# A batch-norm matmul on one core: laying k so that each block of w is one DMA over all partitions, and moving three small products to GpSimd

## The chip, the cores and the metric

One core of a Trainium2 chip. The time is what the device takes for one execution, in microseconds (us), as the median of several. In what follows PE is the matmul engine, DVE the Vector engine, ACT the Scalar engine, GpSimd (POOL in the profile) the engine that also issues the loads of x and w.

## The reference

```python
# x: 16 x 512 x 1024 float32, weight: 1024 x 768
y = np.matmul(x, weight)
mean = np.mean(y, axis=(0, 1), keepdims=True)
var = np.var(y, axis=(0, 1), keepdims=True)
return gamma * (y - mean) / np.sqrt(var + eps) + beta
```

The statistics go over all 8192 rows, so nothing can be written before all of a column's products are there.

## The kernel before

x comes in 16 chunks of 512 rows, cast to bf16 by the DMA. A chunk is loaded in four slabs of 256 columns, each to 32 partitions; DVE then transposes blocks of 32x32 words, where a word is a pair of bf16 values. After that, partition `32 i + c` holds, in block `jw`, the pair of k values that starts at `256 i + 64 jw + 2 c`. w must lie the same way, and since the partition number has two parts with different steps (256 and 2), a block of w takes four DMAs:

```python
def load_w(jw, jw1):
    rows = weight.rearrange("(i jw c e) n -> i c jw (e n)", i=4, jw=JW, e=2)
    dst = w_sb.rearrange("p jw e n -> p jw (e n)")
    for i in range(4):
        seq(nc.gpsimd.dma_start(dst[32 * i:32 * i + 32, jw:jw1], rows[i, :, jw:jw1]))

def turn_x(m0, t0, jw0=0, jw1=JW):
    ...
    src = src.rearrange("p (t jw c) -> p t jw c", jw=JW, c=32)   # 32 words in a row
    ...
    seq(nc.vector.transpose(dst[:, half, :, jw0:jw1], src[:, :, jw0:jw1]))
```

For three of the six column groups most chunks are multiplied with x as the stationary operand (`mm_rows`, 128x384 results). Each such result is squared by ACT, added up by DVE (`add_rows`) and only then copied out by ACT (`keep_rows`), which frees its PSUM bank:

```python
def add_squares(c, s):
    eng, acc = (nc.vector, sum3) if s == RT - 1 and c < C - 3 else (nc.gpsimd, sum2)
    seq(eng.tensor_add(acc, acc, py.pop(("sq", c, s))))

def add_rows(c, s):
    seq(nc.vector.tensor_add(sum1, py["row", c, s][:, 0:NA], sum1))

def keep_rows(c, s):
    ...
    seq(nc.scalar.copy(yrow[c][:, s], py.pop(("row", c, s))[:, 0:NA]))
```

All instructions of an engine run in the order of the kernel's own list of events, so an event's planned time decides its place and nothing else.

## Time and profile before

| | before |
|---|---|
| time, median of 3 | 220.94 us |
| PE busy | 198.5 of 218.9 us |
| DVE busy | 155.7 us |
| a 1024-element transpose (30 of them) | 1.23 us |
| PE's first 128x384 matmul (end of the start) | 24.07 us |
| statistics of the first columns combined, at | 126.48 us |
| statistics of the last column group combined, at | 200.52 us |

The last three rows are landmarks: start, first pass, second pass. They are start times in the timelines of PE and DVE. The lines that show the bound are in the prediction below.

### The profile page before, as it was taken

What the parts mean: (1) busy time and instruction counts of PE and PEld (TensorE: products, weight loads), DVE (VectorE), ACT (ScalarE), POOL (GpSimd) and SP (SyncE); (2) the same over time, 40 slices, a digit from 0 to 9 for tenths busy, and PEclk for the clock granted to TensorE, in tenths of its full rate; (3) what the DMA queues carried; (4) which work ended last, traced back from release to release, by engine and by line L of the source; (5) the groups of instructions that cost most, each with busy time, mean ns of one, the idle gap of its engine ahead of it and who ended that gap; (6) DMA issues with size and microseconds to landing.
All of it is one profiled execution on the core that took longest, in us unless ns stands there. A gap on an engine that the chain in (4) does not pass through costs nothing.

```text
span 218.9 us, 3417 instructions
## 1 busy us (share of the span) xinstructions
PE 198.5 (91%) x1154; PEld 105.2 (48%) x1170; DVE 155.7 (71%) x264; ACT 119.8 (55%) x220; POOL 134.0 (61%) x153
## 2 busy tenths in 40 slices
PE   7998999999999999999999979999999988995900
PEld 3453545454544555546555534444444545651900
DVE  3223788897978789998554287889989999745800
ACT  2001454554543566636666225776676887985850
POOL 8897595977765799935559103999899953000000
PEclk9999999999999999999999999999999999999795
DMA  5999999999999999990000000986769899999698
GB/s 60 175 204 190 194 196 196 197 196 196 194 191 197 195 196 196 198 189 10 0 4 0 0 0 14 340 308 257 269 258 360 295 353 334 346 346 347 201 345 244
DMA packets 70161, 43.75 MB, mean 200 GB/s; under 512 B 4096, under 2 KB 69632, under 8 KB 70144
## 3 DMA queue, kind: packets, MB, share of 16 engines
q0 software_dynamic: 34624, 18.36, 61.1%
q1 hardware_dynamic: 35520, 25.18, 35.7%
q8 instruction: 9, 0.15, 0.3%
q14 instruction: 8, 0.07, 0.1%
HBM read 36.71 MB, written 25.17 MB: 283 GB/s over the span
## 4 chain that ended last, share of the span: by engine, by line
PE 64%; DVE 10%; POOL 8%; DMA 6%; issue 4%; ACT 3%; ACTq 0%; DVEq 0%; POOLq 0%
PE y_ps L190 31%; PE y_ps L180 29%; POOL ring L280 6%; PE o_ps L340 3%; ACT o_sb L353 3%; DVE stats L299 3%; DMA w_sb<-in_weight_dram 3%; DVE ring L274 2%; DVE y_sb L324 2%; DMA ring<-in_x_dram 2%; POOL w_sb L143 2%; DMA out_dram<-ring 1%; POOL ring L156 1%; DVE mv L306 1%; PE a_ps L266 1%
## 5 line engine op out<-in xcount | busy, mean ns | idle before, releaser
L190 PE MATMUL y_ps<-xT_sb,w_sb 128*128 128x512 bf16 (+1 forms) x477 | 117.5, 381 | 2.6 <-DMA w_sb<-in_weight_dram 1.4
L190 PEld LDWEIGHTS <-w_sb 128*128 128x128 bf16 x492 | 46.7, 96 | 60.8 <-issue 3.1
L302 ACT CAST y_sb<-y_ps 128x512 bf16<-128x512 f32 x60 | 35.4, 590 | 53.3 <-DVE stats L299 51.4
L180 PE MATMUL y_ps<-w_sb,xT_sb 128*128 128x384 bf16 x384 | 63.4, 326 | 0.0
L299 DVE BATCH_NORM_STATS2 stats<-y_ps 128x6 f32<-128x512 f32 x60 | 40.6, 684 | 22.5 <-PE y_ps L190 22.3
L280 POOL TENSOR_TENSOR ring<-ring,sum 128x768 f32<-128x768 f32 x24 | 43.5, 1847 | 17.9 <-ACT sum L268 14.0
L156 POOL DMA_DIRECT2D ring<-in_x_dram x72 | 45.2, 633 | 11.7 <-DVE xT_sb L168 6.1
L180 PEld LDWEIGHTS <-xT_sb 128*128 128x128 bf16 x384 | 37.5, 98 | 25.6
L206 POOL TENSOR_TENSOR sum<-sum,sq_sb 128x384 f32<-128x384 f32 x38 | 38.0, 1000 | 18.0 <-ACT sq_sb L202 16.8
L168 DVE STREAM_TRANSPOSE xT_sb<-ring 128x1024 f32<-128x1024 f32 (+1 forms) x34 | 39.5, 1167 | 12.0 <-DMA ring<-in_x_dram 12.0
L340 PE MATMUL o_ps<-ident,y_sb 128*128 128x128 bf16 x240 | 37.3, 230 | 5.5 <-DVE y_sb L324 5.2
L209 DVE TENSOR_TENSOR sum<-y_ps,sum 128x384 f32<-128x384 f32 x48 | 26.1, 544 | 14.6 <-ACT sq_sb L202 13.8
L202 ACT ACTIVATE sq_sb<-y_ps 128x384 f32<-128x384 f32 x48 | 23.4, 492 | 14.9 <-PE y_ps L180 11.4
L215 ACT CAST y_sb<-y_ps 128x384 bf16<-128x384 f32 x48 | 22.9, 476 | 7.5 <-DVE sum L209 7.3
L353 ACT CAST ring<-o_ps 128x1024 f32<-128x1024 bf16 (+1 forms) x24 | 22.5, 960 | 4.9 <-PE o_ps L340 2.5
L340 PEld LDWEIGHTS <-y_sb 128*128 128x128 bf16 x240 | 20.6, 104 | 9.1 <-DVE y_sb L324 7.3
L274 DVE TENSOR_TENSOR ring<-y_sb,a_ps 128x768 f32<-128x768 bf16 x24 | 22.3, 938 | 0.2 <-PE a_ps L266 0.2
L324 DVE TENSOR_SCALAR y_sb<-y_sb,scale,shift 128x512 bf16<-128x512 bf16 x43 | 17.3, 457 | 0.0
L319 ACT ACTIVATE y_sb<-y_sb,shift,scale 128x512 bf16<-128x512 bf16 x17 | 13.3, 813 | 0.1
L149 PE MATMUL idle_ps<-idle_sb 128*128 128x512 bf16 x37 | 9.8, 429 | 1.2 <-DVE idle_sb L100 1.2
L353 ACT CAST o_sb<-o_ps 128x512 f32<-128x512 bf16 x16 | 7.9, 679 | 1.2 <-PE o_ps L340 1.2
L149 PEld LDWEIGHTS <-idle_sb 128*128 128x128 bf16 x38 | 4.0, 108 | 6.4 <-issue 1.9
(45 smaller groups left out, 35.9 us busy)
## 6 DMA issues: line engine op xcount, KB each, us to landing
ring<-in_x_dram POOLq DMA_DIRECT2D x56, 256.0 KB, 8.5
out_dram<-ring SPq DMA_DIRECT2D x32, 384.0 KB, 2.9
out_dram<-ring SPq DMA_DIRECT2D x16, 512.0 KB, 5.9
out_dram<-o_sb SPq DMA_DIRECT2D x16, 256.0 KB, 3.3
ring<-in_x_dram POOLq DMA_DIRECT2D x16, 128.0 KB, 5.2
w_sb<-in_weight_dram POOLq DMA_DIRECT2D x8, 96.0 KB, 4.6
w_sb<-in_weight_dram POOLq DMA_DIRECT2D x4, 192.0 KB, 5.4
gamma_sb<-in_gamma_dram SPq DMA_DIRECT2D x6, 0.5 KB, 4.8
```

What stands on the lines that cost most here:

```text
L156: seq(nc.gpsimd.dma_start(x_bf[32 * i:32 * i + 32], src[:, :, KQ * i:KQ * (i + 1)]))
L168: seq(nc.vector.transpose(dst[:, half, :, jw0:jw1], src[:, :, jw0:jw1]))
L180: seq(nc.tensor.matmul(y_ps, xT[c][:, jw, s * P:(s + 1) * P, e], w_sb[:, jw, e, 0:NA], start=(jw == 0 and e == 0), stop=(jw == JW - 1 and ...
L190: seq(nc.tensor.matmul(y_ps, w_sb[:, jw, e, nt * P:(nt + 1) * P], xT[c][:, jw, q0 * QR:q1 * QR, e], start=(jw == 0 and e == 0 and q0 == 0) ...
L206: seq(eng.tensor_add(acc, acc, py.pop(("sq", c, s))))
L209: seq(nc.vector.tensor_add(sum1, py["row", c, s][:, 0:NA], sum1))
L274: seq(nc.vector.tensor_mul(o_sb, yrow[c][:, s:s + 2], aff[0][:, None, :].to_broadcast([P, 2, NA]),))
L280: seq(nc.gpsimd.tensor_add(o_sb, o_sb, sum1[:, None, :].to_broadcast([P, 2, NA])))
L299: seq(nc.vector.bn_stats(stats[:, nt, i, :], py[nt, c]))
L302: seq(nc.scalar.copy(y(nt, c), py.pop((nt, c))))
L340: seq(nc.tensor.transpose(dst, src, ident))
L353: seq(nc.scalar.copy(o_sb, src))
```

## The change

The intent: with k laid as `8 p + 2 jw + e`, the rows of w that partition p needs follow one another with a single step, so a block is one DMA over 128 partitions. In `turn_x` the 32 words that go to one block no longer lie side by side, but 4 words (16 bytes) apart. With fewer DMAs, blocks 2 and 3 of w are loaded and used one by one. Three 128x128 products move from DVE to GpSimd, and some norms move up by 1 us in the list.

```diff
     def load_w(jw, jw1):
-        rows = weight.rearrange("(i jw c e) n -> i c jw (e n)", i=4, jw=JW, e=2)
+        rows = weight.rearrange("(p jw e) n -> p jw (e n)", jw=JW, e=2)
         dst = w_sb.rearrange("p jw e n -> p jw (e n)")
-        for i in range(4):
-            seq(nc.gpsimd.dma_start(dst[32 * i:32 * i + 32, jw:jw1], rows[i, :, jw:jw1]))
+        seq(nc.gpsimd.dma_start(dst[:, jw:jw1], rows[:, jw:jw1]))
 ...
-        src = src.rearrange("p (t jw c) -> p t jw c", jw=JW, c=32)
+        src = src.rearrange("p (t c jw) -> p t jw c", jw=JW, c=32)
 ...  (shift_diag)
-            seq(nc.vector.tensor_scalar(
+            seq(nc.gpsimd.tensor_scalar(
 ...
-    order = [..., ("w", 1, 2), ("w", 2, 4)]
+    order = [..., ("w", 1, 2), ("w", 2, 3), ("w", 3, 4)]
 ...
-    pe = max(pe, arrive["w", 2])
+    part(2, 0, 2, [2])
+    pe = max(pe, arrive["w", 3])
     for nt in range(NT):
-        unit(nt, 0, MM_US / 2, [2, 3])
+        unit(nt, 0, MM_US / 4, [3])
 ...
-    at(S + 5.2, spread_rows, 1)
+    at(S + 5.0, spread_rows, 1)
 ...
-                at(tb - 2.2 + 0.5 * i, norm, ...)
+                at(tb - 3.2 + 0.5 * i, norm, ...)
```

More of the change, by code (lines that the diff above doesn't have):

```diff
@@ L372 @@
     arrive = {}
-    order = [("x", 0), ("w", 0, 1), ("x", 1), ("w", 1, 2), ("w", 2, 4)]
+    order = [("x", 0), ("w", 0, 1), ("x", 1), ("w", 1, 2), ("w", 2, 3), ("w", 3, 4)]
     order += [("x", q) for q in range(2, SHORT * QPC)] + [("c", c) for c in range(SHORT, C)]
@@ L377 @@
             at(t, load_w, n, *n1)
-            t += 2.1 * (n1[0] - n)
+            t += 1.6
             arrive["w", n] = t + 3.5
@@ L481, in outputs @@
             for i in range(2):
-                at(tb - 2.2 + 0.5 * i, norm, nt, 2 * b + i, "act" if tb < tr + 2.0 and i == 0 else "dve")
+                at(tb - 3.2 + 0.5 * i, norm, nt, 2 * b + i, "act" if tb < tr + 2.0 and i == 0 else "dve")
             at(tb, turn_y, (nt,), 2 * b * CH, 2 * RT)
```

## The prediction

> **What bounds the kernel now.** I first read the page's chain of waits (its shares by engine, then by line), to see which engine carries the end.
>
> ```profile
> PE 64%; DVE 10%; POOL 8%; DMA 6%; issue 4%; ACT 3%; ACTq 0%; DVEq 0%; POOLq 0%
> PE y_ps L190 31%; PE y_ps L180 29%; POOL ring L280 6%; PE o_ps L340 3%; ACT o_sb L353 3%; DVE stats L299 3%; DMA w_sb<-in_weight_dram 3%; DVE ring L274 2%; DVE y_sb L324 2%; DMA ring<-in_x_dram 2%; POOL w_sb L143 2%; DMA out_dram<-ring 1%; POOL ring L156 1%; DVE mv L306 1%; PE a_ps L266 1%
> ```
>
> TensorE's matmuls are the bound; the weight load (3% as DMA, 2% as its issue on GpSimd) is on the chain only at the start. Next, the busy time by stretches (columns: us; busy us and count of PE, PEld, DVE, ACT, POOL; granted clock; DMA share; GB/s).
>
> ```profile
> 13.00:18.70 5.70, 4.44 (x25) 2.21 (x25) 0.89 (x2) 0.00 (x0) 4.66 (x10) 1.00 1.12 201
> 18.70:24.00 5.30, 5.30 (x24) 2.25 (x25) 4.03 (x6) 1.93 (x4) 4.42 (x7) 1.00 1.44 193
> 24.00:45.00 21.00, 20.87 (x111) 10.75 (x111) 17.27 (x24) 10.48 (x23) 15.49 (x21) 1.00 1.45 197
> ...
> 72.00:93.00 21.00, 21.00 (x130) 12.60 (x130) 18.61 (x27) 13.40 (x30) 19.26 (x26) 1.00 1.45 197
> ...
> 126.00:132.00 6.00, 4.74 (x24) 1.83 (x22) 5.39 (x27) 1.35 (x3) 0.00 (x0) 1.00 0.00 0
> ```
>
> From 18.7 us on PE is full until the statistics are combined at 126. But DVE is not far behind: 17.27 of 21 us, then 18.61 of 21. Its slack there is what this change can break. What can be won lies before 18.7, so I read PE's timeline there (start, us, engine, line, what; in brackets the idle time before it and what ended it), and the groups of the two lines that change.
>
> ```profile
> 13.35 4.43 PE L190 MATMUL y_ps<-xT_sb,w_sb 128*128 128x256 bf16 x24 [0.44 <-DVE xT_sb L168]
> 18.66 5.58 PE L190 MATMUL y_ps<-xT_sb,w_sb 128*128 128x512 bf16 x24 [0.88 <-DMA w_sb<-in_weight_dram]
> ...
> L143 POOL DMA_DIRECT2D w_sb<-in_weight_dram x12: 492/508/542, 3.7 to 12.7; - x12
> ...
> L168 DVE STREAM_TRANSPOSE xT_sb<-ring x34: 669/1230/1246, 8.0 to 102.5; 128x1024 f32<-128x1024 f32 x30, 128x512 f32<-128x512 f32 x4
> ```
>
> PE starts the second quarter of x at 13.35, when its transpose is there, works 4.43 us, and then waits only 0.88 us for the last w blocks.
>
> **What the Trainium skill says.** (1) "SBUF — State Buffer", section "Door 1: The DMA port swizzle": SBUF has 16-byte lines, and an engine needs "≥2 hits per line to absorb SRAM access latency"; the same note says strides are free up to 4 fp32. For a stride of exactly 4 fp32, which this change makes, its two halves disagree: one access per line is under two hits, yet four elements is named as free. The trace before has no wide read with such a stride, so it can't decide. (2) The same page, "Who interferes with whom": a Vector instruction in a 2-port mode or with two SBUF inputs shares a port with GpSimd, and the second one waits. The trace agrees: line 312, a 128x1 multiply that takes 0.16 us at 201.66 us with GpSimd idle, takes 1.39 us at 152.02 while GpSimd adds. (3) "DMA: Bandwidth & Descriptors", "Rules for kernel authors": two transfers to disjoint partition halves share the same engines; use one over 128 partitions. That bears on the issue; whether the transfer gets faster no row here shows.
>
> **The change, part by part.**
>
> *Weight load.* Twelve issues of 0.508 us become four: 8 x 0.5 = 4 us less of GpSimd's time in the first 13 us. The program's order shows more: a DMA of GpSimd waits for the one issued eight before it. With fewer DMAs, the second quarter of x and the three later w blocks now wait only for pieces of the first x quarter, all landed by 7.9 us; the last w issue moves from 12.74 to about 8.5. But the landings in the trace show that the engines are already full by then: x0 lands at 7.9 us, w0 at 9.7, x1 at 12.5, w1 at 14.8, w2 and w3 together at 18.5, x2 at 21.3. That is 1.9 us for a w block and 2.7 for an x quarter, in a steady row; only w1 took 0.4 longer. So I expect x1 at 12.3 to 12.5, w2 at about 16.1, w3 at about 18.0. An earlier issue mostly lengthens the wait from issue to landing.
>
> *Blocks 2 and 3 apart.* PE's order of operands is the same by name, but block 2's twelve matmuls (2.8 us) can now go before block 3 is there. PE: 13.35 + 4.43 = 17.8, block 2 to 20.6, block 3 (landed at 18.0) to 23.4, against 18.66 + 5.58 = 24.24. Gain 0.85 us, 1.0 with x1 a little earlier. PE is full from there, so it carries through to the end.
>
> *Transposes.* Same count and shape; the source is read with a step of 4 words (16 bytes) in place of 1. From 669 ns for 512 and 1230 for 1024 elements, an element costs 1.10 ns and the fixed part is 108 ns. If the step is free: nothing changes. If each read takes twice as long: 108 + 2 x 1122 = 2.35 us, 1.1 us more for each. Between 18.7 and 98.4 us (79.7 us) DVE is busy 67.5 us by the stretches (4.03 + 17.27 + 17.83 + 4.65 + 18.61 + 5.12), 28 transposes among it. 28 x 1.1 = 31 more makes 98: 18.6 us more than the stretch has. DVE would become the bound. PE can run ahead of the evictions by the 8 PSUM banks, say 6 of 1.31 us, 8 us, while the last transposes are done by the twelfth chunk: so 10 to 18 us later, about +14, from which the start's 0.9 comes off only in part.
>
> *Shift diagonals on GpSimd.* DVE loses three instructions, 0.67 us at 131.4. PE's order is unchanged, and its matmul for the shift spread runs at 133.8 by its place in that order, not at the 132.0 where the diagonals are done. So 0 to 0.3 us gained; against it GpSimd's three now run from 129.9 on beside the three DVE norms at 130.4, for the first of which PE waits 1.2 us at 130.86: 0 to 0.4 us lost to the shared port. I put the sum at 0.
>
> *Norms 1 us earlier in DVE's order.* PE waits for them 0.69 us at 179.5 and 0.59 at 182.7, so up to 1.3 us; I count 0.4, since DVE is 14.93 of 15 us busy there and something else is pushed back. The last stores run at 346 GB/s from 206 to 217 and start with PE's end, so a shift of PE's end shifts the end.
>
> Sum with a free step: 0.9 + 0.0 + 0.4 = 1.3 us, 220.9 - 1.3 = 219.6.
>
> **Rivals.** (a) *The step halves the transposes' rate and DVE becomes the bound*: 235, between 231 and 239. For it: one access per line, and DVE's small slack. Against it: the note's other half, and that the change is tuned in other places (a lead of 3.2, a spread at 5.0) as one does after seeing it run. (b) *A part penalty*, up to about 1.5 times (0.55 us each, 15 us in all): DVE fills its 12 us of idle time and the PSUM lead takes the rest, so 219.5 to 224. (c) *The weight load gains more*, because one DMA over all partitions uses the write side better: w3 1.5 us sooner, and x1 with it by about 1; PE starts at 12.4 and the gain at the start becomes 2, with the norms' 1.3 in full 3.3: 217.6. Against it: the w pieces land at an even 1.9 us now, faster in bytes than x. (d) *Lost to the port*: the start's gain is eaten by GpSimd against DVE at 130: 220.9.
>
> **Range and chances.** I hold the free or nearly free step at 0.6, (a) at 0.4. Free: 217.5 to 222; (a): 229 to 240. For 8 in 10 the range must reach into (a): 217.8 to 238. The middle is taken inside the likelier group, at its slow side: 220.0. Faster by over 2% (under 216.5) needs more than every part's best case: 0.05. Slower by over 2% (over 225.4) is (a): 0.38. Within: 0.57.
>
> **What will show it.** The group of stream transposes: median 1.23 us (free) or about 2.35 (rival a). In the stretch 24 to 98 us: PE still full, or DVE at 10 tenths and PE waiting for xT or for PSUM evictions. At the start: four w issues of about 0.5 us, w3's landing near 18.0, no wait of PE between the parts, and the first 128x384 matmul near 23.2 instead of 24.07. Near 130: whether the three norms grow from 1.04 us in sum. At 179 to 183: whether PE's two waits shrink. I am wrong if the step costs between 1.5 and 2 times, if the w DMAs land much sooner than their bytes allow for now, or if the moved norms push PSUM evictions so that PE waits for banks.

## The result

233.90 us, median of 4 runs (233.28 to 234.42), against 221.31 us for the kernel before (4 runs): a ratio of 1.0571, 95% interval 1.0525 to 1.0617. Ratios here and below are the mean time of one kernel's runs over that of the kernel before in the same rounds, so they are not quite the ratio of the medians. It is slower by 12.6 us. It lies 13.9 us over the figure that I named, and inside the range only because that range was stretched to reach into the branch that I held for less likely.

First the group of the stream transposes in the changed kernel (minimum, median, maximum in ns; first and last start in us):

```profile
L167 DVE STREAM_TRANSPOSE xT_sb<-ring x34: 1035/2004/2074, 9.0 to 116.6; 128x1024 f32<-128x1024 f32 x30, 128x512 f32<-128x512 f32 x4
```

2004 ns in place of 1230, so 0.77 us more for each. That is neither the free step nor the doubling of the prediction, though it is nearer to the doubling. Next the stretches of the changed kernel, with the same columns as in the prediction:

```profile
18.70:24.00 5.30, 5.30 (x25) 2.26 (x24) 2.20 (x2) 0.00 (x0) 4.18 (x7) 1.00 1.44 193
24.00:45.00 21.00, 19.57 (x105) 10.02 (x105) 19.20 (x23) 11.13 (x24) 12.41 (x17) 1.00 1.33 173
...
72.00:93.00 21.00, 19.15 (x112) 10.74 (x110) 20.62 (x21) 8.54 (x18) 13.97 (x19) 1.00 1.39 182
93.00:98.40 5.40, 4.25 (x25) 2.44 (x25) 5.02 (x7) 3.22 (x8) 4.56 (x6) 1.00 1.36 173
```

Between 72 and 93 us DVE (the third busy time) is full, 20.62 of 21 us; PE is no longer, 19.15, and it got through 112 matmuls where the kernel before got through 130. The list of waits says how DVE holds PE back (who waits, for whom; us in total, times, longest):

```profile
ACT y_sb L214 <- DVE sum L208: 26.4, 21, 2.9
...
PE y_ps L179 <- ACT y_sb L214: 3.5, 5, 0.9
```

In the kernel before, the first of these stood at 7.3 us and the second did not occur. PE waits for a PSUM bank; ACT has to copy the bank out; ACT waits for DVE's `add_rows`; and DVE is in the middle of transposes for later chunks. PE's timeline in that part shows the rhythm (start, us, engine, line, what, and in brackets the idle time before it with what ended it):

```profile
87.05 4.06 PE L179 MATMUL y_ps<-w_sb,xT_sb 128*128 128x384 bf16 x24 [0.94 <-ACT y_sb L214]
91.43 1.46 PE L179 MATMUL y_ps<-w_sb,xT_sb 128*128 128x384 bf16 x8 [0.32 <-ACT y_sb L214]
93.82 4.06 PE L179 MATMUL y_ps<-w_sb,xT_sb 128*128 128x384 bf16 x24 [0.94 <-ACT y_sb L214]
```

The distance between the first and the last of these is 6.77 us, one chunk. The kernel before took 5.2 us for one. DVE's work for such a chunk is two transposes and five adds of 0.545 us; by the durations, which overlap a little, that is 2 x 2.00 + 5 x 0.545 = 6.7 us, about this distance, where it was 2 x 1.23 + 5 x 0.545 = 5.2 us before. And this is what the chain of waits, by engine, has become:

```profile
PE 44%; DVE 27%; issue 11%; ACT 7%; POOL 3%; DMA 3%; DVEq 0%; POOLq 0%; ACTq 0%
```

PE's share fell from 64% to 44%, DVE's rose from 10% to 27%.

Where the time lies, by the landmarks: the first 128x384 matmul starts at 24.08 us (before: 24.07); the first statistics are combined at 138.90 (126.48), which is 12.4 us later; the last ones at 213.58 (200.52), another 0.6 us. So nearly all of the loss is in the first pass. Within it, PE is 1.5 us late when chunk 6 starts (73.45 us, before: 71.97) and 9.75 us late when it sums the statistics (132.35, before: 122.60); the other 2.7 us are lost right there, at the end of the pass.

### The profile page after: what moved, and what is told of

Its sections match the earlier page's. It is cut to its first block, busy times and chain, and to the rows that moved or that the text cites. A ratio compares the mean times of both kernels' runs of the same rounds, so it can differ in the third digit from the quotient of the medians.

```text
span 232.6 us, 3403 instructions
## 1 busy us (share of the span) xinstructions
PE 203.2 (87%) x1154; PEld 105.9 (46%) x1170; DVE 178.9 (77%) x261; ACT 116.5 (50%) x220; POOL 132.9 (57%) x148
## 4 chain that ended last, share of the span: by engine, by line
PE 44%; DVE 27%; issue 11%; ACT 7%; POOL 3%; DMA 3%; DVEq 0%; POOLq 0%; ACTq 0%
PE y_ps L189 29%; PE y_ps L179 11%; DVE xT_sb L167 10%; DVE stats L298 6%; DVE y_sb L323 3%; DMA ring<-in_x_dram 3%; ACT o_sb L352 3%; PE o_ps L339 3%; DVE sum L208 3%; DVE ring L273 2%; ACT sq_sb L201 2%; POOL ring L155 2%; POOL sum L205 1%; DVE sum L205 1%; ACT ring L352 1%
## 5 line engine op out<-in xcount | busy, mean ns | idle before, releaser
L189 PE MATMUL y_ps<-xT_sb,w_sb 128*128 128x512 bf16 (+1 forms) x477 | 119.3, 385 | 3.2 <-DMA w_sb<-in_weight_dram 1.1
L189 PEld LDWEIGHTS <-w_sb 128*128 128x128 bf16 x492 | 47.2, 97 | 64.2 <-issue 6.5
L167 DVE STREAM_TRANSPOSE xT_sb<-ring 128x1024 f32<-128x1024 f32 (+1 forms) x34 | 64.4, 1902 | 15.0 <-DMA ring<-in_x_dram 15.0
L179 PE MATMUL y_ps<-w_sb,xT_sb 128*128 128x384 bf16 x384 | 65.1, 326 | 6.9 <-ACT y_sb L214 3.5
L298 DVE BATCH_NORM_STATS2 stats<-y_ps 128x6 f32<-128x512 f32 x60 | 40.0, 682 | 16.6 <-PE y_ps L189 16.4
L214 ACT CAST y_sb<-y_ps 128x384 bf16<-128x384 f32 x48 | 23.4, 488 | 26.4 <-DVE sum L208 26.4
L352 ACT CAST ring<-o_ps 128x1024 f32<-128x1024 bf16 (+1 forms) x24 | 23.0, 985 | 3.3 <-PE o_ps L339 2.2
L323 DVE TENSOR_SCALAR y_sb<-y_sb,scale,shift 128x512 bf16<-128x512 bf16 x43 | 20.5, 531 | 0.0
```

What stands on the lines that cost most here:

```text
L179: seq(nc.tensor.matmul(y_ps, xT[c][:, jw, s * P:(s + 1) * P, e], w_sb[:, jw, e, 0:NA], start=(jw == 0 and e == 0), stop=(jw == JW - 1 and ...
L189: seq(nc.tensor.matmul(y_ps, w_sb[:, jw, e, nt * P:(nt + 1) * P], xT[c][:, jw, q0 * QR:q1 * QR, e], start=(jw == 0 and e == 0 and q0 == 0) ...
L298: seq(nc.vector.bn_stats(stats[:, nt, i, :], py[nt, c]))
L352: seq(nc.scalar.copy(o_sb, src))
```

## The experiments

Theory 1 is rival (a) of the prediction: the step makes the transposes slow, and DVE becomes the bound.

### The transposes read in a row again, all else changed

```diff
-        src = src.rearrange("p (t c jw) -> p t jw c", jw=JW, c=32)
+        src = src.rearrange("p (t jw c) -> p t jw c", jw=JW, c=32)
```

> The changed kernel with one thing undone: the stream transposes read their source word after word again, so the result is wrong on purpose; the weight DMAs, the shift diagonals on GpSimd and the early norms stay. Theory 1 (the step of 16 bytes alone makes the transposes slow and DVE the bound): median of a 1024-element transpose back at 1.23 us, PE without waits from 24 to 126 us, time 219 to 221. Rival 2 (the wider weight DMAs, which landed x0 1 us later in the profile, or the other parts cost it): transposes 1.23 us but the time stays over 228.

221.49 us, ratio 1.0018 (0.9982 to 1.0053), 0.5 us over the range that I expected and equal to the kernel before; the result is wrong, as intended. The transposes are back:

```profile
L167 DVE STREAM_TRANSPOSE xT_sb<-ring x34: 668/1231/1246, 8.8 to 103.1; 128x1024 f32<-128x1024 f32 x30, 128x512 f32<-128x512 f32 x4
```

This one word order is the whole difference: 233.9 - 221.5 = 12.4 us. The wide DMAs, the split of the blocks, GpSimd's products and the early norms together come to nothing.

### Only the layout, on the kernel before

The kernel before with the new `load_w` and the new word order in `turn_x`, nothing else.

> The kernel before with nothing but the layout: one DMA over 128 partitions per load of w (three loads, blocks 2 and 3 together), transposes with the step of 16 bytes. Right result. Theory 1: the whole loss is here, 232 to 235, transposes at 2.0 us. Rival: part of the loss comes from the shift diagonals and early norms, then 230 or less.

232.0 us, ratio 1.0462 (1.0398 to 1.0526); transposes at a median of 2012 ns. Most of the loss is here without the other parts. It is 1.9 us below the changed kernel, so beside slow transposes those other parts cost something. The profiles place about half of it at the start. With blocks 2 and 3 apart, as in the changed kernel, DVE gets the first results of chunk 0 at 23.7 us, here at 19.6; it then takes them together with the slow transposes of chunk 1, and PE waits 1.29 us in the changed kernel for the second of these (1.38 us with the step of 8 words below), here 0.35. With quick transposes, in the run above, PE does not wait there. The early norms cost another 0.6 us, as shown below.

### A step of 2 words, and of 8

If the cost comes from the lines of 16 bytes that the prediction cites, a step of 8 bytes should be free, and one of 32 should cost no more than one of 16. For the step of 2, k is laid as `256 i + 128 h + 4 c + 2 j + e`, with four DMAs for each block of w, and the result is right:

```diff
-        src = src.rearrange("p (t c jw) -> p t jw c", jw=JW, c=32)
+        src = src.rearrange("p (t h c j) -> p t h j c", h=2, j=2, c=32)
```

> As e3_all_but_layout, but with k laid so that the transposes read with a step of 2 words (8 bytes)[...]. Right result. If the cost is that of fetching a new 16-byte line for each read (two reads per line hide it): transpose median 1.23 us, time within 0.5 us of e3_all_but_layout. If the cost grows with the step: about 1.5 us each, DVE fills its idle time, time 1 to 4 us over e3_all_but_layout.

For the step of 8 only the duration counts:

```diff
-        src = src.rearrange("p (t c jw) -> p t jw c", jw=JW, c=32)
+        src = src.rearrange("p (tt c j) -> p tt j c", j=8, c=32)
```

> The changed kernel with a step of 8 words (32 bytes) in the transposes; result wrong on purpose; only the duration matters. If the cost is one new 16-byte line per read, a longer step costs no more: median 2.0 us as with 16 bytes. If the cost grows with the step: 2.5 us or more.

The two groups, the step of 2 first:

```profile
L170 DVE STREAM_TRANSPOSE xT_sb<-ring x34: 670/1232/1247, 8.0 to 106.0; 128x1024 f32<-128x1024 f32 x30, 128x512 f32<-128x512 f32 x4
```

```profile
L167 DVE STREAM_TRANSPOSE xT_sb<-ring x34: 1067/2042/2080, 8.0 to 116.8; 128x1024 f32<-128x1024 f32 x30, 128x512 f32<-128x512 f32 x4
```

1231 ns for a step of 1 word, 1232 for 2, 2004 for 4, 2042 for 8. That is a threshold between 8 and 16 bytes, and it fits one rule: two reads from a line cost nothing extra, one read from a line does. It does not fit a cost that grows with the step. That the lines are the cause is the reading of the page cited in the prediction; the runs show the threshold. A step of 3 words, which could tell lines of 16 bytes from a plain limit on the step, was not tried.

### The wide DMA undone, the step kept

The changed kernel with w loaded by four DMAs for each block:

```diff
-        rows = weight.rearrange("(p jw e) n -> p jw (e n)", jw=JW, e=2)
+        rows = weight.rearrange("(i c jw e) n -> i c jw (e n)", i=4, jw=JW, e=2)
```

> The changed kernel, its layout and its step of 16 bytes kept, but each block of w loaded by four DMAs of 32 partitions. Right result. Theory 1: as slow as the changed kernel, 233 to 235, since the DMAs do not matter and the step does. Rival 2 (the single wide DMA is at fault): 220 to 224.

234.95 us, ratio 1.0618 (1.0556 to 1.068): as slow as the changed kernel, with transposes at 2006 ns. The wide DMA is not at fault.

### Everything but the layout

The changed kernel with both `rearrange` lines and the four DMAs of the kernel before.

> Everything of the change except the layout of k: w in four DMAs of 32 partitions per block again, blocks 2 and 3 still apart, shift diagonals on GpSimd, norms 1 us earlier. Right result. Theory 1: 219.5 to 221.5, with PE's first 128x384 matmul about 0.8 us earlier than 24.07. Rival 2 (the other parts cost something, as the changed kernel lost 1.3 us after its statistics were combined): 222 to 224.

224.19 us, ratio 1.0136 (1.0079 to 1.0193). This misses what Theory 1 said (219.5 to 221.5) and lies 0.2 us over the rival's band (222 to 224), for another reason than the rival's. PE's timeline at the end of the start:

```profile
26.91 6.91 PE L180 MATMUL y_ps<-w_sb,xT_sb 128*128 128x384 bf16 x32 [2.68 <-DVE xT_sb L168]
```

PE waits 2.68 us for the next part of x. The line shows a second loss: its 32 matmuls take 6.91 us in place of 5.36, for the granted clock fell to 0.50 for 3.4 us as the wait ended. Splitting blocks 2 and 3 without the wide DMA makes sixteen loads of w in place of twelve, about 0.5 us of GpSimd's time each, and the loads of x stand behind them. Between 18.7 and 24 us the DMA moved 117 GB/s, where the kernel before moved 193. So the split needs the wide DMA, and an experiment that undoes one half of a pair does not measure the other half alone. The step of 2 words (224.1 us, ratio 1.0126) has the same four DMAs for a block, a like wait (2.20 us) and the same halved clock after it, so it is rightly compared with this kernel, and there it is equal.

### Which chunks carry the loss

The step only in chunks 5 to 15, then only in chunks 0 to 4; the rest reads in a row. Their outputs are wrong, which doesn't matter for the times.

```diff
-        src = src.rearrange("p (t c jw) -> p t jw c", jw=JW, c=32)
+        src = src.rearrange(
+            "p (t c jw) -> p t jw c" if c >= 5 else "p (t jw c) -> p t jw c", jw=JW, c=32)
```

> The changed kernel with the step of 16 bytes only in the transposes of chunks 5 to 15 (22 instructions), chunks 0 to 4 read word after word; result wrong on purpose. Theory 1 with DVE as the bound where its work per chunk is over PE's time per chunk (after about 66 us): most of the loss stays, 228 to 233. If the loss is in proportion to the number of slow transposes (22 of 32 halves): 229. If the start carries it: under 225.

> The reverse: the step of 16 bytes only in chunks 0 to 4 (4 half-size and 8 full transposes), the others word after word; result wrong on purpose. Theory 1: the early chunks take PE 10.6 us each, DVE has room for 0.77 us more per transpose, so almost nothing is lost past the first two chunks: 221.5 to 223.5. In proportion: 225 or more.

Late chunks: 229.58 us, ratio 1.0355 (1.0286 to 1.0425), 8.1 over the kernel that reads in a row. Early chunks: 223.04 us, ratio 1.0066 (0.999 to 1.0141), 1.6 over it; against the kernel before that is not clear of noise. Per chunk that is 0.74 and 0.31 us, so the late ones do weigh more, though 229.58 is also about what the count alone would give: the late run by itself does not tell the two apart, the early run does (225 or more was the count's figure). The parts make 9.7 and not 12.4 us: early slow transposes use up DVE's spare time, and late ones then find less of it. The profiles bear this out: PE's first wait for a PSUM bank comes at 81.8 us with all transposes slow, and at 89.7 with the late ones alone. The early run's loss shows in PE's timeline as one wait of 1.27 us for the second half of chunk 1.

### Less work for DVE, in both kernels

If DVE's work sets the pace, then any work taken from it must help the changed kernel and not the kernel before. The add of squares that DVE does once per chunk (ten times 0.55 us) is left out; the variance is wrong.

```diff
+        if s == RT - 1 and c < C - 3:
+            py.pop(("sq", c, s))
+            return
-        eng, acc = (nc.vector, sum3) if s == RT - 1 and c < C - 3 else (nc.gpsimd, sum2)
+        eng, acc = nc.gpsimd, sum2
```

> The changed kernel with less work for DVE: the one add of squares per chunk that DVE does (0.55 us each) is left out, so the variance is wrong on purpose. Theory 1 (DVE's work, not a single late transpose, sets PE's pace between 70 and 120 us): about ten of them lie before 122 us, most in the stretch where PE waits, so 3 to 6 us come off: 228 to 231. If PE waited only for the transposes of its own chunk: within 1 us of the changed kernel.

> The same adds left out of the kernel before; variance wrong on purpose. Theory 1: DVE has time to spare there, so nothing comes off, 221 to 222 beside the kernel before.

The changed kernel: 228.97 us, 4.9 us less for 5.5 us of work. (In its profile PE starts on the sums of the statistics 3.9 us earlier, at 128.50; the rest may be the clock, which was not halved after that here, as it was in the changed kernel.) The kernel before: 221.45 us, ratio 0.9977 (0.9904 to 1.0051), nothing. The same stretch, 72 to 93 us, first the changed kernel without those adds, then the kernel before without them:

```profile
72.00:93.00 21.00, 20.06 (x122) 11.71 (x121) 20.24 (x21) 10.05 (x23) 15.99 (x22) 1.00 1.42 190
```

```profile
72.00:93.00 21.00, 21.00 (x129) 12.39 (x128) 17.03 (x24) 13.28 (x30) 19.11 (x25) 1.00 1.45 195
```

In the first, DVE is still full and PE gained ten matmuls (122 for 112). In the second, DVE only idles more and PE does what it did. This is the clearest sign that DVE's work sets the pace in the one and not in the other.

### The two smaller parts alone

Only the shift diagonals on GpSimd, then only the early norms, each on the kernel before.

```diff
-            seq(nc.vector.tensor_scalar(aff["diag"][:, 1, a], ...
+            seq(nc.gpsimd.tensor_scalar(aff["diag"][:, 1, a], ...
```

```diff
-                at(tb - 2.2 + 0.5 * i, norm, ...)
+                at(tb - 3.2 + 0.5 * i, norm, ...)
```

> The kernel before with only the three shift diagonals on GpSimd. Right result. My prediction said 0, between 0.3 us gained and 0.4 lost: 221 to 222 beside the kernel before, from the combined statistics to PE's end 74.0 us as before (all runs with the old tail show 74.04, all with the new one 74.7). If the diagonals carry the 0.65 us lost there: 74.7.

> The kernel before with only the norms 1 us earlier in the order. Right result. My prediction gave it 0.4 us of gain. What the profiles now suggest: the norms, moved in among GpSimd's last adds, wait for the shared port (0.45 us becomes 1.4 to 2.2), so that from the combined statistics to PE's end it takes 74.7 us in place of 74.04, and the time is 0.5 to 0.8 us over the kernel before.

Diagonals: 221.31 us, ratio 0.999 (0.9966 to 1.0014), and 74.1 us from the first combined statistics to the last (before: 200.52 - 126.48 = 74.0). No effect. Norms: 222.38 us, ratio 1.0044 (1.0013 to 1.0074), and 74.6 us: a loss of 0.6 us there. All profiles agree: 74.0 to 74.1 us with the old places of the norms (four kernels), 74.6 to 74.7 with the new ones (ten). DVE's timeline in the early-norm run shows what happened to two of the norms:

```profile
165.10 1.81 DVE L324 TENSOR_SCALAR y_sb<-y_sb,scale,shift 128x512 bf16<-128x512 bf16 x1
...
171.01 1.39 DVE L324 TENSOR_SCALAR y_sb<-y_sb,scale,shift 128x512 bf16<-128x512 bf16 x1
```

In the kernel before, the first four norms of this part took 0.40 to 0.45 us each. The single records of the trace say why: in both kernels all four of these norms end 0.15 to 0.21 us after one of GpSimd's adds ends, as if each had waited for the add. In their old places they start 0.2 to 0.3 us before such an end; the two above start 0.2 and 0.6 us after an add has begun.

But only about 0.2 of the 0.6 us is lost there. In the kernel before, two small steps behind the norms waited instead (1.18 and 1.68 us, here 0.44 and 0.16), and DVE comes to its line 313 at 176.13 us (before: 176.23). What differs is how PE waits after that. The kernel before:

```profile
179.47 0.23 PE L340 MATMUL o_ps<-ident,y_sb 128*128 128x128 bf16 x1 [0.69 <-DVE y_sb L324]
182.70 0.68 PE L340 MATMUL o_ps<-ident,y_sb 128*128 128x128 bf16 x5 [0.59 <-DVE y_sb L324]
```

and with the norms early:

```profile
180.88 0.22 PE L340 MATMUL o_ps<-ident,y_sb 128*128 128x128 bf16 x1 [0.84 <-DVE ring L274]
184.27 0.22 PE L340 MATMUL o_ps<-ident,y_sb 128*128 128x128 bf16 x1 [0.50 <-ACT y_sb L302]
186.10 0.22 PE L340 MATMUL o_ps<-ident,y_sb 128*128 128x128 bf16 x1 [0.32 <-ACT ring L353]
```

The waits for norms, 1.28 us in all, are gone, but 1.66 us of other waits have come, two of them, by the profile, for ACT to copy out a PSUM bank. ACT itself waited there for DVE's statistics (1.42 us before its copy at 183.63; in the kernel before at most 0.93), which stood behind two norms.

### A try at a better version

To keep the wide DMA with a step of only 2 words, k can be laid as `512 h + 4 p + 2 j + e`, with x loaded in runs of 512 bytes:

```diff
-        src = x_flat[m0:m0 + rows].rearrange("(t r) k -> r t k", r=32)
+        src = x_flat[m0:m0 + rows].rearrange("(t r) (h i q) -> i r t h q", r=32, h=2, i=4)
```

> A try at keeping the single w DMA without the slow step: k laid as 512 h + 4 p + 2 j + e, so that w is one DMA over all partitions per block and the transposes step by 2 words only; the price is that x is loaded in runs of 512 bytes in place of 1 KB. Blocks 2 and 3 apart; shift diagonals and norms as before. Right result. If the x loads keep their rate (193 GB/s written): transposes 1.23 us, start 0.5 to 1 us earlier, 220.5 to 221.5. If they pay for twice as many pieces: below 150 GB/s from 24 to 98 us, PE waits for x, 230 or more.

It did not build: such a load has four dimensions on one side, and the build refused more than three. Two loads for each slab would double GpSimd's issues for x, which the four-DMA runs show to be dear. No kernel here beats the kernel before.

## Why the prediction was right or wrong

- **What bounds the kernel, and what could break.** Right. PE was the bound, and DVE's small slack between 24 and 98 us was what the change could break, and did.
- **The step of 16 bytes.** Undecided in the prediction, and its likelier branch (0.6 for a free step) was the wrong one, and with it the figure of 220.0. The step costs 1.63 times, in the gap between 1.5 and 2 that I had named as being wrong. Of the note in "SBUF — State Buffer", section "Door 1: The DMA port swizzle", the half about two hits per line held, the half that counts four fp32 as free did not (2004 ns against 1232 for two). I let an argument about how the change must have come about outweigh it; that argument had no number in it.
- **The size of rival (a).** The mechanism was right, but terms of the sum were off. The step costs 0.77 us and not 1.1. With 0.77, my own sum gives 67.5 + 28 x 0.77 = 89.1 us, 9.4 over the stretch, less 8 for the lead of PSUM: only about 1.4 us, where the statistics came 12.4 us later. The failing step is the one that rival (b) puts into words, "DVE fills its 12 us of idle time and the PSUM lead takes the rest". The last transpose starts at 116.6 us in place of 102.5, 14.1 us later for 30 x 0.77 = 23.1 us of work: DVE gave up 9 us of idle time, less than the 12.2 that I had counted. The lead then gave back 4.4 us and not 8: PE comes to the sums of the statistics 9.75 us late. The other 2.7 us come from two things that I had not seen: PE waits 0.97 us for GpSimd's late adds of squares, and right after, its clock is halved. The stretches of the changed kernel around 136 us:

```profile
133.00:135.00 2.00, 1.03 (x8) 0.79 (x8) 0.25 (x1) 0.59 (x1) 0.99 (x1) 0.96 0.00 0
135.00:138.00 3.00, 3.00 (x8) 1.01 (x7) 0.00 (x0) 0.00 (x0) 0.00 (x0) 0.50 0.00 0
```

  Eight matmuls in 3 us is half their pace, at a granted clock of 0.50. Records of the clock put it at 3.4 us, so 1.7 us lost. Rival (a)'s 14 us came out near 12.4 only because the errors cancelled.
- **The start.** Right, and hidden. The first transpose began at 8.96 us and not 7.99, for x0 landed late; that happened in kernels with the old DMAs too (8.8 us in the one without the layout, 8.0 in the one with the layout alone), so it is not the change. Counted from the first transpose to the first 128x384 matmul, the kernel before takes 16.1 us, the one that reads in a row 14.8 (8.80 to 23.60), the changed kernel 15.1. One pair says little, for the same stretch is 14.8 to 15.7 us in the six profiles with the new start and 15.7 to 16.7 in the four with the old one: about 0.9 us on average, where I had said 0.85 to 1.0. As said, the earlier issue only lengthened the wait to landing. The issues of w in the kernel before (KB each, median us to landing):

```profile
w_sb<-in_weight_dram POOLq DMA_DIRECT2D x8, 96.0 KB, 4.6
w_sb<-in_weight_dram POOLq DMA_DIRECT2D x4, 192.0 KB, 5.4
```

  and in the changed kernel:

```profile
w_sb<-in_weight_dram POOLq DMA_DIRECT2D x4, 384.0 KB, 8.7
```

- **Shift diagonals.** Right: 0. GpSimd needs 1.99 us for the three, DVE 0.67, and PE's place in the order hides both.
- **Norms.** Wrong in sign. I counted 0.4 us gained; they cost 0.6. The step that failed is that PE's two waits would shrink: 1.28 us of waits became 1.66, partly for PSUM banks, which was the last of my signs of being wrong. Two of the moved norms waited for GpSimd's adds (1.81 and 1.39 us), as the port rule of "Who interferes with whom" has it, which I had used for the diagonals at 130 us; but all save 0.2 us of that delay was made up before PE's waits.
- **Rivals (b), (c) and (d).** (b)'s size was too small, 0.77 us a transpose against its 0.55; its sum was not tried at its own size, but at 0.77 the same sum falls short by 11 us, as shown above. (c): the wide DMA moved no faster; it saves issue time only. (d) did happen in effect, through the norms and not the diagonals: in the kernel that reads in a row, the gain of the start is gone at the end.

## What to carry to other kernels

When a layout is changed for the sake of a DMA, look at the step it gives the other end. Here a step of 16 bytes in place of 8 or 4 decided whether thirty transposes took 2.0 or 1.23 us each, while the DMA's gain was about 1 us in all. Before an engine off the path is given more work, compare its work with the pace per chunk and not over a whole stretch, and test it from the other side by taking work away. An instruction moved up in an engine's order may meet another engine's lock, and pushes back what stood there before.

## What the Trainium skill lacked or had wrong

- "SBUF — State Buffer", section "Door 1: The DMA port swizzle": the note on lines names 4 fp32 as a free step. For the 32x32 transpose of 4-byte words on DVE a step of 2 words is free (1232 ns), and steps of 4 and 8 cost 1.63 and 1.66 times as much (2004 and 2042 ns). The note's own condition of two hits per line gives this; its list does not. The note also gives no size for the penalty on DVE: 0.77 us for 1024 words, 0.75 ns a word.
- "GPSIMD Engine Reference", section "4.1 Engine selection": one-input work on GpSimd is called roughly line-rate. Three products of 128x128 took 1.99 us on it and 0.67 on DVE, three times as long at this small size.
- "DMA: Bandwidth & Descriptors", "Rules for kernel authors": the advice to use one transfer over all partitions holds for the issue (four loads and 2.3 us of GpSimd's time in place of twelve and 6.1), but the runs show no faster transfer, and the page gives no figure for what small loads, issued first, cost the loads behind them: PE waited 2.2 to 2.7 us for x in the three runs with sixteen loads of w.
- "TensorE: Matmul & The Clock Gate", section "What's actually happening", tells of half clock after an idle window of about 3.4 us. Here the granted clock fell to 0.50, mostly for 3.4 us, after waits of 0.95, 0.97 and 1.48 us between small 128x1 matmuls in three profiles, and not after waits of 0.75 to 0.95 us at the same place in three others; it fell at waits for x of 2.20 and 2.68 us, and not at one of 2.72. So the length of the wait alone does not decide it; what does stays open.
